# Scores as one float32 product each, and two more projection units in seven products: a neighbourhood-attention layer on one Trainium2 core

## The chip, the cores and the metric

The kernel runs on one core of one Trainium2 chip, in one launch. The metric is the device time of that launch in microseconds. The engines are named as the profile names them: PE (matrix products), PEld (loading of a product's stationary operand), DVE (vector), ACT (scalar activation), POOL (GpSimd), SP (the queue that issues most DMAs).

## The reference

One layer of a transformer trunk over 2048 tokens of width 1024 that form a grid of 32 rows by 64 columns: RMS norm, one input projection into queries, keys, values and a gate, 2-D neighbourhood attention with 16 heads of 64, SiLU gate, output projection, residual, final RMS norm. All is float32.

```python
h = rmsnorm(x, norm_0)
q, k, v, gate = split(h @ w_in_0, 4)                  # 2048 x 1024 each
# query (r, c) sees 8 rows x 16 columns of keys around it, clipped at the border
s = q . k / sqrt(64) + rpb[head, row offset, column offset]
o = softmax(s) @ v
x = x + (o * silu(gate)) @ w_out_0
out = rmsnorm(x, norm_f)
```

## The kernel before

**Products.** Large products run as three float32r products, high by high, high by low and low by high: an operand is copied into float32r by ACT (the high half) and the difference to the copy is formed by DVE (the low half). The `o` products of attention (L1123) take float32 operands whole.

**Stage one** projects the first 1024 tokens, **stage two** the other 1024. A block of columns of queries, keys or gate (a unit: 256 output columns, 1024 tokens) is either made by `group` (L378 to L382: per 128 columns and 512 tokens 8 x 3 products, 96 for a unit's 1024 tokens) or by `seven_products` (L434): a Strassen-like scheme with 7 instead of 8 block products, 7 x 12 = 84 products, and additions on DVE (`s`, `u`, `tmp`). Values are made by `values_of` (L555). Before, stage two does six units with seven products (`units_two`); the other six (`halves`) are made by `group` later, as filling between attention's steps.

**Stores between stages.** `give` takes a finished block. Queries go to `qd`, the gate through tanh to `sgd`. Of keys ACT makes a high copy (L364) and DVE the low rest (L365), and both are stored, in `k_hi` and `k_lo`. `store` puts a DMA into a list with a due time that is counted in products (`clock`); `due` issues what has come due.

**The attention stage** has 32 cycles, one for each pair of heads p and row tile T (8 x 64 queries). `order` gives first all pairs with T = 0, then each pair with T = 1 and 2, then all with T = 3. The keys of a tile span 11, 15, 15 and 12 rows. In cycle m PE runs, in this order: some filling products (`feed`), the transposes of the last cycle's probabilities (`turns`, L1101), two calls of `scores` (L1021) and two of `values` (L1123, tile `o`). `scores` handles a pair of column blocks; for each column block and each of the two heads, which sit in the lower and upper 64 partitions, it computes

```python
for m, (qq, kk) in enumerate(((qh, kh), (qh, kl), (ql, kh))):
    for s in range(2):
        a = slice(s * 64, s * 64 + 64)
        nc.tensor.matmul(pst[s], qq[a, qs], kk[a, :r1 - r0, c0:c1].rearrange("p r (s c) -> p s r c", c=8), ...)
```

Then DVE adds the bias table and takes the row maximum (L1029), ACT takes the exponential (L1035), DVE the reciprocal of the sums (L1040), and `normalise` multiplies on POOL (L1044). The bias tables `em` are sums made on POOL (L987). `split_q` (L519, L520) makes the halves of the queries, scaled by 1/8, from the loaded tile `qr`.

**Filling.** `amount[m]` is the number of products that `feed` takes in cycle m: 28 in the first 25 cycles, the rest spread over the last seven. The filling is first `projections` (the remaining units by `group`), then `outputs` (L1322 to L1326), the output projection, whose operand rows are split by `split_og` (L1187, L1188). `consume` splits the next weights on ACT and DVE (L189, L190).

Of the kernel before, what the change touches and what calls it, by code (L numbers as in the profile page):

```python
# [70 lines left out]
def build(ctx, tc, x, xr, xt, wg, rpb, last, w_out, n0, nf, masks, out):  # L71
# [4 lines left out]
    k_hi = [dram.tile([128, S], F32, name=f"k_hi{p}") for p in range(NP)]  # L76
    k_lo = [dram.tile([128, S], F32, name=f"k_lo{p}") for p in range(NP)]
# [53 lines left out]
    rt = one.tile([128, 16], F32, name="rt")  # L131
    g0 = one.tile([128, NK], F32, name="g0")
# [25 lines left out]
    def load_item(it):  # L158
        kind, a, b = it
        t = raws[it] = raw([128, 512], F32, "raw")  # L160
        asked_at[it] = clock[0]
# [44 lines left out]
    def stats(c):  # L206
        ss = rows.pop(c)
        m = tiny.tile([128, 8], F32, name="m")[:, :4]
        nc.vector.tensor_tensor(m, ss[:, 0:8:2], ss[:, 1:8:2], OP.add)
        nc.vector.tensor_scalar(m, m, 1.0 / D, EPS, op0=OP.mult, op1=OP.add)  # L210
        rsqrt(rt[:, 4 * c:4 * c + 4], m, 4)

# [32 lines left out]
    units_two = [(k, j) for j in range(2) for k in "kqg"]  # L245
    halves = [(k, j, 1, c) for j in range(2, 4) for g in (("k", "q", "g") if j == 2 else ("k", "qg")) for c in (2, 3) for k in g]
# [16 lines left out]
    clock = [0.0]  # L263
    freed = set()
# [23 lines left out]
    def consume(n, asked=False, turn=False):  # L288
        for _ in range(n):
            load_ahead()  # L290
            if attending[0] and not asked and not turn:
                return
            if state["used"] == len(items) or not may_use(items[state["used"]]):
                return
            if attending[0] and clock[0] - asked_at[items[state["used"]]] < 32 and not asked:
                return
            it = items[state["used"]]
            state["used"] += 1
            use_item(it)
# [44 lines left out]
    def give(kind, hp, c, t, bank_=False):  # L344
        while sum(e[1][0] in "kqg" for e in later) > 1:
            later.pop(0)[2]()
        s = slice(c * 512, c * 512 + 512)
        written.add((kind, hp, c))
        to, at = (lambda o: lay(kind, o), of(kind, t)) if bank_ else (lambda o: o, t)
        if kind == "g":  # L350
            sg = ev([128, 512], F32, "sg")
            nc.scalar.activation(to(sg), at, AF.Tanh, scale=0.5)
            nc.vector.scalar_tensor_tensor(to(sg), to(sg), 1.0, at, op0=OP.add, op1=OP.mult)
            store(("g", hp, c), 12, lambda: nc.sync.dma_start(sgd[hp][:, s], sg))
            return
        if kind == "q":
            if bank_:
                t = ev([128, 512], F32, "q")
                nc.scalar.activation(to(t), at, AF.Copy)
            store(("q", hp, c), 12, lambda: nc.sync.dma_start(qd[hp][:, s], t))  # L360
            return
        hi = ev([128, 512], F32R, "hi")
        lo = ev([128, 512], F32R, "lo")
        nc.scalar.activation(to(hi), at, AF.Copy)  # L364
        nc.vector.tensor_tensor(to(lo), at, to(hi.bitcast(F32)), OP.subtract)  # L365
        store(("k", hp, c), 12, lambda: (nc.sync.dma_start(k_hi[hp][:, s], hi.bitcast(F32)),
                                         nc.sync.dma_start(k_lo[hp][:, s], lo.bitcast(F32))))
# [20 lines left out]
    def evac_v(u, t, p):  # L388
        v = ev([128, 512], F32, "v")
        nc.scalar.activation(v, p, AF.Copy, scale=rt[:, t:t + 1] if t < 8 else 1.0)  # L390
# [140 lines left out]
    def split_v(u, a, b, ks=(0, 1)):  # L531
        t = VR[u, a, b].rearrange("p (k c) -> p k c", c=256)
        if a == 0 and ks[0] == 0:
# [3 lines left out]
        nc.scalar.activation(h, t[:, k], AF.Copy)  # L537
# [28 lines left out]
    def stage_one():  # L566
# [119 lines left out]
        for k in range(NK):  # L686
            if k == 0:
                for h in range(2):
                    split_to(*(t[:, parts_[h]] for t in X1["B11"][0]), land["x11"][0][:, parts_[h]], gain("x11", 0))
                    if h == 0:  # L690
                        split_v(0, 0, 0, (0,))
                        split_v(0, 1, 0, (0,))
# [93 lines left out]
    def stage_two():  # L786
# [9 lines left out]
        def also(n, i):  # L796
            if n == 0:
# [12 lines left out]
                if i == 3:  # L810
                    for f in load_k(0, 0) + [load_q(0, 0)]:
                        f()
                if i == 5:
                    split_q(0, 0)
# [117 lines left out]
    def load_k(p, T):  # L932
# [3 lines left out]
        KT[p, T] = []  # L936

        def keys(src):
            t = kp([128, 960], F32R, "kt")
            KT[p, T].append(t.rearrange("p (r c) -> p r c", c=GW))  # L940
            nc.sync.dma_start(t[:, :n].bitcast(F32), src[p][:, r0 * GW:r1 * GW])

        return [lambda: keys(k_hi), lambda: keys(k_lo)]

    def load_q(p, T):
        must(("q", p, T))

        def queries():
            QT[p, T] = t = lp([128, 512], F32, "qr")
            nc.sync.dma_start(t, qd[p][:, T * 512:T * 512 + 512])  # L950

        return queries

    def split_q(p, T):
        t = QT[p, T]
        QT[p, T] = h, l = qp([128, 512], F32R, "qh"), qp([128, 512], F32R, "ql")
        split_to(h, l, t, HD ** -0.5)
# [50 lines left out]
    def scores(i, between=None):  # L1008
        p, T, cs = pairs[i]
        kh, kl = KT[p, T]  # L1010
        qh, ql = QT[p, T]
        r0, r1 = KEY_ROWS[T]
        got = []
        for C in cs:
# [3 lines left out]
            for m, (qq, kk) in enumerate(((qh, kh), (qh, kl), (ql, kh))):  # L1018
                for s in range(2):
                    a = slice(s * 64, s * 64 + 64)  # L1020
                    nc.tensor.matmul(pst[s], qq[a, qs], kk[a, :r1 - r0, c0:c1].rearrange("p r (s c) -> p s r c", c=8), start=(m == 0), stop=(m == 2))  # L1021
# [16 lines left out]
    def normalise(i):  # L1038
        st = ST.pop(i)
        nc.vector.reciprocal(st[:, 8:12], st[:, 4:8])  # L1040
        for j, C in enumerate(pairs[i][2]):
            for s in range(2):
                o = 8 + 2 * j + s
                nc.gpsimd.tensor_scalar(X[i, C][s], X[i, C][s], st[:, o:o + 1], 0.5, op0=OP.mult, op1=OP.mult)  # L1044
# [236 lines left out]

    def outputs():
        loaded_at = {1: -1e9}
# [5 lines left out]
        def ahead(k, i=0):  # L1289
            n = ready["loaded"]  # L1290
            if n < tiles and place[n] <= k + 4 and og_ready(n):
                load_og(n)
                loaded_at[n] = clock[0]
# [4 lines left out]
            near = 2 if quiet[0] else -1  # L1298
            if n < ready["loaded"] and place[n] <= k + near and clock[0] - loaded_at[n] >= 28 and whole(n):
# [38 lines left out]
    dense, end_of_it = 28.0, 24  # L1338
# [3 lines left out]
    amount[1] += first  # L1342
    calm_debt = dense / 4
# [34 lines left out]
    def begin(m):  # L1378
# [6 lines left out]
        if m + 1 < cycles:  # L1385
            nx = order[m + 1]
            if nx[1] == 3:
                later_loads(load_last(nx[0]), 12, 1.5)
            later_loads(load_k(*nx), 14 if nx[1] < 3 else 22, 5)
# [3 lines left out]

    def middle(m):
        if 1 <= m < cycles:
            split_q(*order[m])
        if m + 1 < cycles:
            later_loads([load_q(*order[m + 1])], 1, 0)
# [12 lines left out]
    for m in range(cycles + 1):  # L1411
        a = amount[m]
        begin(m)
        feed(a * 0.35)
        if m:
            normalise(2 * m - 1)
        middle(m)
        if m:
            quiet[0] = True
            for k in range(3):  # L1420
                consume(1 + (m == 1), turn=True)
                feed(a * 0.11)
# [4 lines left out]
            if quiet[0]:  # L1427
                consume(1, turn=True)
                feed(a * 0.12)
                quiet[0] = False  # L1430
            else:
                feed(a * 0.12)
        else:
            feed(a * 0.45)
        feed(a * 0.2, 8)
# [12 lines left out]
        if m:  # L1448
            values(2 * m - 2)
            values(2 * m - 1)  # L1450
        n = next_sums(m)
# [55 lines left out]
```

## Time and profile before

| | |
|---|---|
| median of 3 runs | 1062.33 us (1062.28 to 1062.53) |
| the profiled execution's own time | 1062.42 us |
| span of its trace | 1060.6 us |
| PE busy | 1048.6 us, 99% of the span |
| DVE, ACT, POOL busy | 725.7, 518.5, 312.9 us |
| granted TensorE clock, mean | 0.999 |
| DMA | 207.58 MB, 196 GB/s |
| attention stage | from about 531 us to about 1005 us |

The trace covers the span; some 1.8 us of the profiled execution lie outside it. Busy shares are averages over stages; what bounds a stage is read from PE's timeline and from what PE waits for.

### The profile page before, as it was taken

What the parts mean: (1) busy time and instruction counts of PE and PEld (TensorE: products, weight loads), DVE (VectorE), ACT (ScalarE), POOL (GpSimd) and SP (SyncE); (2) the same over time, 40 slices, a digit from 0 to 9 for tenths busy, and PEclk for the clock granted to TensorE, in tenths of its full rate; (3) what the DMA queues carried; (4) which work ended last, traced back from release to release, by engine and by line L of the source; (5) the groups of instructions that cost most, each with busy time, mean ns of one, the idle gap of its engine ahead of it and who ended that gap; (6) DMA issues with size and microseconds to landing.
All of it is one profiled execution on the core that took longest, in us unless ns stands there. A gap on an engine that the chain in (4) does not pass through costs nothing.

```text
span 1060.6 us, 20997 instructions
## 1 busy us (share of the span) xinstructions
PE 1048.6 (99%) x7608; PEld 877.1 (83%) x7608; DVE 725.7 (68%) x1593; ACT 518.5 (49%) x1218; POOL 312.9 (30%) x392
## 2 busy tenths in 40 slices
PE   8999999999999999999999999999999999999997
PEld 6888888887888888888888888888887888888886
DVE  5476888768897625666576667766778777686654
ACT  7645344333343334333265656666767656445422
POOL 0000221322311000000157775665756642213200
PEclk9999999999999999999999999999999999999999
DMA  8733655353635433533798778886987788777352
GB/s 309 227 100 108 190 202 179 126 149 119 184 120 154 120 100 89 170 99 129 234 300 262 239 238 246 269 268 207 297 280 251 222 282 273 255 243 247 105 155 80
DMA packets 129184, 207.58 MB, mean 196 GB/s; under 512 B 11768, under 2 KB 55544, under 8 KB 129080
## 3 DMA queue, kind: packets, MB, share of 16 engines
q1 hardware_dynamic: 128648, 205.84, 62.5%
q8 instruction: 60, 0.98, 0.4%
q10 hardware_dynamic: 432, 0.40, 0.1%
q14 instruction: 44, 0.36, 0.1%
HBM read 147.47 MB, written 58.72 MB: 194 GB/s over the span
## 4 chain that ended last, share of the span: by engine, by line
PE 91%; DVE 4%; issue 1%; POOL 1%; DMA 1%; ACT 0%; SPq 0%; POOLq 0%; DVEq 0%
PE pp L434 30%; PE pv L555 16%; PE s L1021 7%; PE o L1123 7%; PE po L1324 5%; PE po L1326 5%; PE po L1322 5%; PE pp L382 4%; PE pp L378 4%; PE pp L380 4%; PE ph L1101 4%; DVE f L417 1%; POOL x L1044 1%; DMA land<-in_xt_dram 1%; POOL em L987 1%
## 5 line engine op out<-in xcount | busy, mean ns | idle before, releaser
L1044 POOL TENSOR_SCALAR x<-x,st 128x360 f32<-128x360 f32 (+5 forms) x256 | 176.1, 706 | 222.9 <-DVE st L1040 205.0
L434 PE MATMUL pp<-h,f 128*128 128x512 f32 x576 | 186.6, 390 | 0.0
L1035 ACT ACTIVATE x<-x,st 128x360 f32<-128x360 f32 (+5 forms) x256 | 151.3, 593 | 23.7 <-DVE st L1029 23.7
L454 POOL TENSOR_TENSOR tmp<-tmp,rb 128x512 f32<-128x512 f32 x36 | 58.6, 1628 | 270.1 <-DVE tmp L452 209.4
L987 POOL TENSOR_TENSOR em<-e,mk 128x264 f32<-128x264 f32 (+3 forms) x94 | 78.0, 864 | 192.1 <-DMA mk<-in_masks_dram 189.4
L434 PEld LDWEIGHTS pp<-h,f 128*128 128x128 f32 x576 | 108.2, 188 | 22.2
L1029 DVE CUSTOM_DVE_ANT_0 x<-s,em 128x360 f32<-128x360 f32 (+5 forms) x256 | 123.8, 538 | 0.6 <-POOL em L987 0.6
L434 PE MATMUL pp<-t,f 128*128 128x512 f32 x480 | 121.7, 390 | 0.3
L434 PE MATMUL pp<-l,f 128*128 128x512 f32 x288 | 112.2, 389 | 0.0
L434 PEld LDWEIGHTS pp<-t,f 128*128 128x128 f32 x480 | 90.0, 188 | 19.6 <-DVE u L447 1.1
L1324 PE MATMUL po<-woh,gl 128*128 128x512 f32 x252 | 99.2, 394 | 1.5 <-DVE gl L1188 1.5
L1326 PE MATMUL po<-wol,gh 128*128 128x512 f32 x252 | 98.9, 393 | 0.0
L1322 PE MATMUL po<-woh,gh 128*128 128x512 f32 x252 | 98.9, 393 | 0.0
L1077 DVE COPY pta<-ph 120x512 f32<-120x512 f32 (+5 forms) x96 | 57.8, 641 | 55.4 <-PE ph L1101 55.4
L555 PE MATMUL pv<-wh,h 128*128 128x512 f32 x256 | 88.4, 391 | 1.9 <-ACT h L519 1.4
L555 PE MATMUL pv<-wh,l 128*128 128x512 f32 x256 | 88.2, 390 | 0.0
L555 PE MATMUL pv<-wl,h 128*128 128x512 f32 x256 | 88.2, 390 | 0.0
L1077 ACT ACTIVATE pta<-ph 120x512 f32<-120x512 f32 (+5 forms) x96 | 49.7, 558 | 77.0 <-PE ph L1101 76.8
L1123 PEld LDWEIGHTS o<-pta,vt 120*64 120x64 f32 (+2 forms) x1792 | 80.9, 138 | 7.4 <-DVE st L1029 5.4
L1123 PE MATMUL o<-pta,vt 120*64 120x128 f32 (+5 forms) x1792 | 85.3, 253 | 0.0
L417 DVE TENSOR_TENSOR f<-raw,f 128x512 fp32r<-128x512 f32 x90 | 69.7, 775 | 22.4 <-ACT f L416 22.4
L1021 PE MATMUL s<-kt,qh 64*128 64x480 f32 (+5 forms) x512 | 83.0, 372 | 0.5 <-DVE pta L1077 0.5
(157 smaller groups left out, 1959.5 us busy)
## 6 DMA issues: line engine op xcount, KB each, us to landing
raw<-in_wg_dram SPq DMA_DIRECT2D x126, 256.0 KB, 5.0
row<-in_xr_dram SPq DMA_DIRECT2D x32, 256.0 KB, 4.0
vd<-v SPq DMA_DIRECT2D x32, 256.0 KB, 2.4
k_hi<-hi SPq DMA_DIRECT2D x32, 256.0 KB, 2.5
k_lo<-lo SPq DMA_DIRECT2D x32, 256.0 KB, 2.9
sgd<-sg SPq DMA_DIRECT2D x32, 256.0 KB, 4.1
qr<-qd SPq DMA_DIRECT2D x32, 256.0 KB, 5.0
sgt<-sgd SPq DMA_DIRECT2D x32, 256.0 KB, 5.1
```

Source lines behind the costliest of these rows:

```text
L434: nc.tensor.matmul(B[n, P], t[:, int(m == 2), c], x[k][int(m == 1)], start=P in (1, 6, 5) and k == 0 and m == 0, stop=k == 3 and m == 2, s ...
L555: nc.tensor.matmul(ps[t], a[:, o], b, start=k == 0 and m == 0, stop=k == NK - 1 and m == 2)
L987: (nc.gpsimd if attending[0] or not s else nc.vector).tensor_tensor(sh(t), E[p, s][:, u0 + 4:u1 + 4, v0 + 8:v1 + 8].rearrange("p u (s v) - ...
L1021: nc.tensor.matmul(pst[s], qq[a, qs], kk[a, :r1 - r0, c0:c1].rearrange("p r (s c) -> p s r c", c=8), start=(m == 0), stop=(m == 2))
L1029: nc.vector.tensor_tensor_reduce(X[i, C][s], pst[s], EM[p, ROW_TYPE[T], COL_TYPE[C], s], -1.0, 1e38, OP.add, OP.min, st[:, o:o + 1])
L1035: nc.scalar.activation(X[i, C][s], X[i, C][s], AF.Exp, bias=st[:, o:o + 1], scale=-1.0, accum_out=st[:, 4 + o:5 + o])
L1044: nc.gpsimd.tensor_scalar(X[i, C][s], X[i, C][s], st[:, o:o + 1], 0.5, op0=OP.mult, op1=OP.mult)
L1077: (nc.vector.tensor_copy if h else lambda o, i_: nc.scalar.activation(o, i_, AF.Copy))(t[:k, h, b * 512:b * 512 + w], banks_[b, h][:k, :w])
L1123: nc.tensor.matmul(to.rearrange("d (h q) -> d h q", q=64) if nq > 64 else to, vt[:k, strip, s * 64:s * 64 + 64], t[:k, h, at:at + 64] if n ...
L1322: nc.tensor.matmul(p, gh, woh[q, j], start=(i == 0), stop=False)
L1324: nc.tensor.matmul(p, gl, woh[q, j], start=False, stop=False)
L1326: nc.tensor.matmul(p, gh, wol[q, j], start=False, stop=(i == NK - 1))
```

## The change

- `scores`: one float32 product for each column block and head, in place of three float32r products. Keys and queries stay whole: one store `kd`, one load per tile; `split_q` and `middle` go; queries are scaled by 1/8 when they are stored.
- Stage two: eight units by `seven_products` (`k` and `q` of the third column are added), so four by `group` in the attention stage. The filling of the first 25 cycles falls from 28 to 20.3 products a cycle (plus or minus 1.5 in turn in cycles 8 to 23).
- `normalise` of the second pair multiplies its second column block on ACT. The factor 0.5, which stood in that multiply, moves into the store of the values (`rth`).
- The cycle feeds 10 products before that `normalise`, and the rest in other shares. The rows of the output projection are split by `split_rows` in the quiet places of a cycle, at most three turns ahead.
- Start: DVE in place of ACT converts one of the first value weights; two loads are cut in halves and interleaved with those of x.
- Times of loads are counted with `now()`, which adds 26 products for each cycle run.

```diff
-    units_two = [(k, j) for j in range(2) for k in "kqg"]
-    halves = [(k, j, 1, c) for j in range(2, 4) for g in (("k", "q", "g") if j == 2 else ("k", "qg")) for c in (2, 3) for k in g]
+    units_two = [(k, j) for j in range(2) for k in "kqg"] + [(k, 2) for k in "kq"]
+    halves = [(k, j, 1, c) for j in range(2, 4) for g in (("g",) if j == 2 else ("k", "qg")) for c in (2, 3) for k in g]
...
+        if bank_:
+            t = ev([128, 512], F32, kind)
+            nc.scalar.activation(to(t), at, AF.Copy, scale=HD ** -0.5 if kind == "q" else 1.0)
+        elif kind == "q":
+            nc.scalar.activation(t, t, AF.Copy, scale=HD ** -0.5)
+        store((kind, hp, c), 12, lambda: nc.sync.dma_start((qd if kind == "q" else kd)[hp][:, s], t))
...
         for b in (1, 2, 3):
-            for a in range(2):
-                load_v0(0, a, b, ev([128, 512], F32, "raw") if b == 3 else None)
-            for k in (2 * b, 2 * b + 1):
-                load("x%d1" % (k // 4 + 1), k % 4)
+            for j in range(2):
+                for a in range(2):
+                    if b == 1:
+                        load_v0(0, a, b, cols=parts_[j])
+                    elif j == 0:
+                        load_v0(0, a, b, ev([128, 512], F32, "raw") if b == 3 else None)
+                load("x%d1" % (b // 2 + 1), (2 * b + j) % 4)
...
-            for m, (qq, kk) in enumerate(((qh, kh), (qh, kl), (ql, kh))):
-                for s in range(2):
-                    a = slice(s * 64, s * 64 + 64)
-                    nc.tensor.matmul(pst[s], qq[a, qs], kk[a, :r1 - r0, c0:c1].rearrange("p r (s c) -> p s r c", c=8), start=(m == 0), stop=(m == 2))
+            for s in range(2):
+                a = slice(s * 64, s * 64 + 64)
+                nc.tensor.matmul(pst[s], qt[a, qs], kt[a, :r1 - r0, c0:c1].rearrange("p r (s c) -> p s r c", c=8), start=True, stop=True)
...
-                nc.gpsimd.tensor_scalar(X[i, C][s], X[i, C][s], st[:, o:o + 1], 0.5, op0=OP.mult, op1=OP.mult)
+                if both and j:
+                    nc.scalar.activation(X[i, C][s], X[i, C][s], AF.Copy, scale=st[:, o:o + 1])
+                else:
+                    nc.gpsimd.tensor_scalar(X[i, C][s], X[i, C][s], st[:, o:o + 1], 1.0, op0=OP.mult, op1=OP.mult)
...
+    def split_rows():
+        n = ready["split"]
+        if n < ready["loaded"] and "turn" in ready and place[n] <= ready["turn"] + 3 and now() - late["loaded_at"][n] >= 40 and whole(n) \
+                and sum(1 if hasattr(g, "rearrange") else 2 for g in G.values()) <= 6:
+            split_og(n)
+            ready["split"] += 1
+            return True
...
-    dense, end_of_it = 28.0, 24
+    dense, end_of_it = 20.3, 24
...
+    for m in range(8, 24):
+        amount[m] += 1.5 if m % 2 == 0 else -1.5
...
+            later_loads([load_q(*nx), load_k(*nx)], 7, 5)
...
-        a = amount[m]
+        a = amount[m] - 10
         begin(m)
-        feed(a * 0.35)
+        feed(10)
         if m:
-            normalise(2 * m - 1)
-        middle(m)
+            normalise(2 * m - 1, True)
         if m:
             quiet[0] = True
             for k in range(3):
-                consume(1 + (m == 1), turn=True)
-                feed(a * 0.11)
+                if not split_rows():
+                    consume(1 + (m == 1), turn=True)
+                feed(a * 0.17)
```

More of the change, by code (lines that the diff above doesn't have):

```diff
@@ L75, in build @@
     qd = [dram.tile([128, S], F32, name=f"qd{p}") for p in range(NP)]
-    k_hi = [dram.tile([128, S], F32, name=f"k_hi{p}") for p in range(NP)]
-    k_lo = [dram.tile([128, S], F32, name=f"k_lo{p}") for p in range(NP)]
+    kd = [dram.tile([128, S], F32, name=f"kd{p}") for p in range(NP)]
     sgd = [dram.tile([128, S], F32, name=f"sgd{p}") for p in range(NP)]
@@ L131, in build @@
     rt = one.tile([128, 16], F32, name="rt")
+    rth = one.tile([128, 8], F32, name="rth")
     g0 = one.tile([128, NK], F32, name="g0")
@@ L263, in build, with now @@
     clock = [0.0]
+    runs = [0]
+    def now():
+        return clock[0] + 26 * runs[0]
     freed = set()
@@ L294, in consume @@
                 return
-            if attending[0] and clock[0] - asked_at[items[state["used"]]] < 32 and not asked:
+            if attending[0] and now() - asked_at[items[state["used"]]] < 36 and not asked:
                 return
@@ L935, in load_k, with keys @@
         must(*[("k", p, c) for c in range(r0 // 8, (r1 + 7) // 8)])
[L936 to L943, printed above, removed]
+        def keys():
+            t = kp([128, 960], F32, "kt")
+            KT[p, T] = t.rearrange("p (r c) -> p r c", c=GW)
+            nc.sync.dma_start(t[:, :n], kd[p][:, r0 * GW:r1 * GW])
+        return keys
     def load_q(p, T):
@@ L1036, in scores, with normalise @@
                                      accum_out=st[:, 4 + o:5 + o])
-    def normalise(i):
+    def normalise(i, both=False):
         st = ST.pop(i)
@@ L1297, in ahead @@
             n = ready["split"]
-            near = 2 if quiet[0] else -1
-            if n < ready["loaded"] and place[n] <= k + near and clock[0] - loaded_at[n] >= 28 and whole(n):
+            ready["turn"] = k
+            if ended[0] and n < ready["loaded"] and place[n] <= k + 2 and now() - loaded_at[n] >= 28 and whole(n):
                 split_og(n)
@@ L1450, in build @@
             values(2 * m - 1)
+        runs[0] += 1
         n = next_sums(m)
```

72 lines of the change are left out of this document (27 added, 45 removed).

## The prediction

> **What bounds the kernel now.** I read the page first: the busy times and the chain that ended last.
>
> ```profile
> span 1060.6 us, 20997 instructions
> PE 1048.6 (99%) x7608; PEld 877.1 (83%) x7608; DVE 725.7 (68%) x1593; ACT 518.5 (49%) x1218; POOL 312.9 (30%) x392
> PE 91%; DVE 4%; issue 1%; POOL 1%; DMA 1%; ACT 0%; SPq 0%; POOLq 0%; DVEq 0%
> ```
>
> PE is 99% busy and is 91% of the chain. So the time is the sum of what PE streams, plus the few places where PE waits. I therefore read PE's own timeline, start to start, because ends are modelled. Columns: start us, length us.
>
> ```profile
> 606.61 0.39 PE L382 MATMUL pp<-h,w 128*128 128x512 f32 x1
> 612.51 0.39 PE L380 MATMUL pp<-l,w 128*128 128x512 f32 x1
> 612.82 1.43 PE L1101 MATMUL ph<-ident,x 64*88 64x64 f32 x44
> 614.06 0.55 PE L1021 MATMUL s<-kt,qh 64*128 64x264 f32 x3
> 616.42 2.67 PE L1123 MATMUL o<-pta,vt 88*64 88x128 f32 x56
> 619.01 0.51 PE L382 MATMUL pp<-h,w 128*128 128x512 f32 x1
> 665.65 0.74 PE L1021 MATMUL s<-kt,qh 64*128 64x360 f32 x4
> 668.56 0.66 PE L1123 MATMUL o<-pta,vt 120*64 120x128 f32 x8
> 894.62 0.71 PE L1021 MATMUL s<-kt,qh 64*128 64x288 f32 x4
> 897.12 2.67 PE L1123 MATMUL o<-pta,vt 96*64 96x128 f32 x56
> ```
>
> Between the first two rows lie 26 float32r products: 5.90/26 = 0.227 us each, 0.443 ns per column. A score block (all four column blocks of one head pair and row tile) takes 616.42 - 614.06 = 2.36 us where the tile has 11 key rows, 668.56 - 665.65 = 2.91 us with 15, and 897.12 - 894.62 = 2.50 us with 12. There are 8, 16 and 8 such blocks: 18.9 + 46.6 + 20.0 = 85.4 us. The block of `o` products takes 619.01 - 616.42 = 2.59 us, and the transposes 614.06 - 612.82 = 1.24 us.
>
> Where PE waits is in the waits by engine (total us, times, longest):
>
> ```profile
> PE po L1324 <- DVE gl L1188: 1.5, 2, 1.1
> PE pv L555 <- ACT h L519: 1.4, 1, 1.4
> PEld pp L434 <- DVE u L447: 1.1, 2, 0.6
> ```
>
> So little is to be won from waits. The change is decided by PE's own work.
>
> **Two more units by seven products.** `units_two` grows from six to eight. A unit costs 7 x 12 = 84 products in this form and 96 in `group`. That is 2 x 12 = 24 products less, at 0.227 us: -5.4 us. The additions that it costs instead lie on DVE, which has room where that stage runs; I cost them at nothing.
>
> **The scores.** Each is one float32 product where there were three float32r products. No float32 score is in this trace, so I need a price from other float32 work. The products by form show how many records one product leaves (count | busy us, mean ns):
>
> ```profile
> L1021 PE MATMUL s<-kt,qh 64*128 64x480 f32 x128 | 25.1, 417 | 0.4 <-DVE pta L1077 0.4
> L1021 PE MATMUL s<-kt,ql 64*128 64x480 f32 x64 | 18.5, 412 | 0.0
> L1123 PE MATMUL o<-pta,vt 120*64 120x128 f32 x512 | 38.9, 276 | 0.0
> ```
>
> The 16 blocks with 15 key rows have 4 scores of 480 columns each, 64 in all: 192 records, three per score, one per float32r product. The `o` products are float32 already. The same 16 blocks hold 16 of 128 columns each, 256 in all, and leave 512 records: two passes per float32 product.
>
> One `o` block has 16 products of 128 columns and 12 of 64, spread over two halves of the output's partitions that run side by side. Each half therefore streams 16 x 128 + 12 x 64 = 2816 columns in its two passes, in 2.59 us: 0.920 ns per column and pass, 2.08 times the 0.443 of float32r. A second row is the transposes, float32 in one pass on the two halves of the input's partitions, as the scores are: 22 x 64 = 1408 columns in 1.24 us, 0.881 ns. The two agree, with switching between blocks included.
>
> A head's score block has 112 key columns times 11, 15 or 12 rows: 1232, 1680 and 1344 columns. Two passes at 0.920 make 2.27, 3.09 and 2.47 us against 2.36, 2.91 and 2.50 now. With 8, 16 and 8 blocks that is 18.1 + 49.5 + 19.8 = 87.4 us, +1.9. At the transposes' 0.881 the blocks would take 2.17, 2.96 and 2.37 us, 83.7 us in all: -1.7, the lower bound.
>
> The upper bound comes from how slowly float32r runs in this place now:
>
> ```profile
> 666.28 0.82 PE L1021 MATMUL s<-kt,qh 64*128 64x480 f32 x4
> 667.03 0.81 PE L1021 MATMUL s<-kt,qh 64*128 64x480 f32 x4
> ```
>
> From the first score block of 480 columns to the second, 0.75 us pass for three products per head: 0.521 ns per column, where 0.443 is paid elsewhere. Something here (runs of eight keys, or two streams at once) stretches a pass. If a float32 product costs four such passes, the blocks grow by one third of what lies in them: 0.521 x 1232, 1680 and 1344 ns = 0.64, 0.88 and 0.70 us, or 8 x 0.64 + 16 x 0.88 + 8 x 0.70 = +24.8 us. I take +1.9: both float32 rows are near it, and a stretch of a stream that runs at half speed has time to hide.
>
> The Trainium skill (FP8 and Floating Point Precision, TensorE Precision Notes) says that true FP32 takes four passes through the array. The two records at 2.08 times the float32r column agree with that, 4.16 in all. By that rule with each pass priced as a score pass now, the sum would be the upper bound and not +1.9.
>
> **What becomes lighter beside PE.** Key halves and query halves are no longer formed, and the low halves are neither stored nor loaded:
>
> ```profile
> L365 DVE TENSOR_TENSOR lo<-tmp,hi 128x512 fp32r<-128x512 f32 x22 | 15.0, 682 | 5.5 <-ACT hi L364 5.5
> L520 DVE SCALAR_TENSOR_TENSOR ql<-qr,qh 128x512 fp32r<-128x512 f32 x32 | 26.1, 815 | 16.9 <-ACT qh L519 14.1 <-DMA ogd<-og 2.0 <-DMA e<-in_rpb_dram 0.3
> L519 ACT ACTIVATE qh<-qr 128x512 fp32r<-128x512 f32 x32 | 19.8, 618 | 0.0
> k_lo<-lo SPq DMA_DIRECT2D x32, 256.0 KB, 2.9
> 280.00:320.00 40.00, 40.00 (x178) 33.13 (x178) 37.26 (x51) 14.76 (x26) 9.84 (x6) 1.00 0.44 134
> ```
>
> All this lies beside PE, so its direct worth is nothing. The last row (a window: PE, PEld, DVE busy) shows DVE at 37.26 of 40 us in the first seven-product stage; without `lo` it has slack, and I let the waits of PE behind `u` go: -0.6 us. ACT now scales the queries, where the first stage stored them as they came; it is busy 14.76 of 40 there and hides that. SP issues one key load per block instead of two; the load of queries moves from 1 to 7 products into a cycle and that of keys from 14 to 12, both for the cycle after, so nothing near waits for them.
>
> **The start.** The change cuts the two loads of the second value weights in halves, and puts the second halves behind the next tile of x. ACT works in order, and `split_v` of these weights stands before the split of that tile.
>
> ```profile
> 9.93 0.63 ACT L537 ACTIVATE wh<-raw 128x512 fp32r<-128x512 f32 x1 [1.43 <-DMA raw<-in_wg_dram]
> 11.41 1.41 ACT L519 ACTIVATE h<-land,g 128x512 fp32r<-128x512 f32 x2 [0.85 <-DMA land<-in_xt_dram]
> 12.18 1.20 PE L555 MATMUL pv<-wh,h 128*128 128x512 f32 x4 [1.38 <-ACT h L519]
> ```
>
> Now x lands last, at 11.41, and PE starts 0.77 us later. After the change weights land last, at about the same time, since the bytes are the same, and one or two weight splits of 0.63 us stand between that and x: +0.6 to +1.3, or -0.7 if half the bytes of a load decide. I take +0.7. The earlier first product (DVE takes one of the first conversions) ends in this same wait and is worth nothing.
>
> **The dense cycles.** In 25 cycles of the attention stage 20.3 products fill the time between the blocks instead of 28; the total stays, since two units moved ahead. So each cycle is 7.7 x 0.227 = 1.75 us shorter, and ACT, DVE and POOL have that much less time. Two of eight `normalise` multiplies per cycle move to ACT.
>
> ```profile
> 638.70:858.10 219.40, 217.39 (x2444) 186.28 (x2441) 161.14 (x434) 144.59 (x378) 135.22 (x173) 1.00 0.82 252
> L1044 POOL TENSOR_SCALAR x<-x,st 128x480 f32<-128x480 f32 x64 | 52.0, 826 | 11.8 <-DVE st L1040 10.7
> ```
>
> The 16 cycles of the window take 13.7 us each, with DVE 10.1, ACT 9.0 and POOL 8.5 busy. After it a cycle is 13.7 - 1.75 + 0.18 = 12.1; DVE loses 0.8 (`ql`), ACT loses 0.6 and gains some 1.2, POOL loses two multiplies of 0.83: 9.3, 9.6, 6.8 at most. All fit. PE's 2.0 us of waits there include the 1.5 behind `gl`; the output rows are now split earlier (two ACT copies and two DVE subtractions each, in place of a weight split), so I let these 1.5 go and set 1.5 against them for cycles with less slack: nothing in sum.
>
> **Sum.** -5.4 + 1.9 - 0.6 + 0.7 = -3.4 us. The profiled execution took 1062.4 us (span 1060.6), 0.1 above the median 1062.3. So 1059.0 against it, and 1058.9 as a median. About 0.2%, 2.1 us, is what a measurement of this kernel can tell from no change.
>
> **Rivals.** *Stretched passes (slower).* Float32 scores carry the stretch of float32r in this place. For it: the same operands in the same runs of eight, and 0.521 against 0.443. Against it: the transposes use the same input halves at 0.881. In full it gives -3.4 + 24.8 - 1.9 = +19.5, 1082; with half the difference 1070. It decides from +1.9 + 3.4 = 5.3 us more than now, 6% on the block. The Trainium skill (SBUF — State Buffer, SBUF: two separate sides) says that a read wants two hits per 16-byte line; runs of eight float32 meet that, which speaks against this rival, but no run here shows it.
>
> *A late normalise (slower).* The transposes wait for `normalise`, which now waits in ACT's queue behind the exponentials and a fill's evacuation.
>
> ```profile
> 655.12 0.33 PE L1123 MATMUL o<-pta,vt 120*64 120x128 f32 x2
> 658.40 0.58 ACT L1035 ACTIVATE x<-x,st 128x360 f32<-128x360 f32 x1
> 661.49 2.64 POOL L1044 TENSOR_SCALAR x<-x,st 128x480 f32<-128x480 f32 x4 [2.17 <-DVE st L1040]
> 664.33 1.39 PE L1101 MATMUL ph<-ident,x 64*120 64x64 f32 x39
> ```
>
> Exponentials end 3.9 us after the scores; two multiplies on POOL (1.7) reach 5.6; PE gets to the transposes after 2.59 + 20.3 x 0.227 = 7.2, against 9.2 here. Slack 1.6 us; in this cycle POOL began 2.5 us after the exponentials, which would overrun it by 0.9. If half of 25 cycles do: +11, 1070.
>
> *Better than forecast.* Transposes' price for the scores, and the 1.5 us behind `gl` won without new waits: -3.4 - 3.6 - 1.5, 1054.
>
> **Chances.** Forecast 0.50, stretched passes 0.24, late normalise 0.14, better 0.12. The forecast's own spread (1056 to 1062) puts a quarter of it within 0.2%. So faster 0.48, same 0.15, slower 0.37. The range takes the better case and both rivals at half price: 1053 to 1074; stretched passes in full are left out. The forecast's own range is 1056 to 1062.
>
> **What would show it.** Score blocks of about 2.27, 3.09 and 2.47 us, with two records per score. 24 products fewer in stage two and the fill. PE's first long wait some 0.7 us longer, none behind `gl`. Transposes that follow the fill without a gap. The prediction is wrong if score blocks exceed 3.3 us with 15 key rows, or if PE's busy share in the dense cycles falls below 97%.

## The result, and the profile after

The changed kernel took 1074.6 us (median of 5 runs, 1069.29 to 1075.61) against 1062.28 (1061.06 to 1062.53) for the kernel before: a ratio of 1.0111, interval 1.0086 to 1.0137. It is slower; the forecast was 1058.9. The profiled execution took 1075.17 us, its span 12.3 us more than before.

The page of the changed kernel, busy times and shares of the chain:

```profile
span 1072.9 us, 20176 instructions
PE 1053.9 (98%) x7328; PEld 859.5 (80%) x7328; DVE 699.3 (65%) x1556; ACT 535.5 (50%) x1254; POOL 256.1 (24%) x328
PE 92%; DVE 3%; ACT 2%; issue 1%; DMA 1%; SPq 0%; DVEq 0%; ACTq 0%
```

PE runs 280 fewer instructions and is busy 5.3 us longer. DVE and POOL are busy less, as predicted; no engine became the bound. Summed from PE's timeline, from the start of one record to the start of the next, so that a wait ahead of a block counts to what ran before it:

| us | before | after | |
|---|---|---|---|
| products of queries, keys, gate | 479.1 | 472.5 | -6.6 |
| products of values | 176.0 | 176.9 | +0.9 |
| scores | 87.1 | 101.7 | +14.7 |
| transposes | 41.5 | 46.2 | +4.7 |
| `o` products | 83.0 | 83.1 | 0 |
| output rows (`po`) | 180.2 | 179.3 | -0.9 |
| other products (`zp`, `prb`) | 6.1 | 5.8 | -0.3 |

The waits of PE (total us, times, longest):

```profile
PE s L1019 <- DVE pta L1078: 5.3, 2, 4.5
PE s L1019 <- DVE y L1221: 2.9, 1, 2.9
PE pv L559 <- ACT h L520: 1.4, 2, 1.2
PE zp L124 <- DVE z L121: 1.2, 1, 1.2
PE s L1019 <- DVE sg L360: 1.2, 1, 1.2
PE po L1333 <- DVE gl L1189: 0.6, 1, 0.6
```

The wait behind `gl` has shrunk from 1.5 to 0.6. New are waits ahead of or inside score blocks, 9.4 us in all and all for DVE. Undisturbed score blocks, from PE's timeline (start, length):

```profile
642.91 2.58 PE L1019 MATMUL s<-kt,q 64*128 64x264 f32 x16
645.42 2.67 PE L1124 MATMUL o<-pta,vt 88*64 88x128 f32 x56
...
714.16 3.17 PE L1019 MATMUL s<-kt,q 64*128 64x360 f32 x16
717.26 0.99 PE L1124 MATMUL o<-pta,vt 120*64 120x128 f32 x16
...
1001.22 2.72 PE L1019 MATMUL s<-kt,q 64*128 64x288 f32 x16
1003.87 0.88 PE L1124 MATMUL o<-pta,vt 96*64 96x128 f32 x14
```

A block takes 2.51 us with 11 key rows, 3.10 with 15 and 2.65 with 12; eight scores leave 16 records, two each. All 32 blocks at these lengths are 20.1 + 49.6 + 21.2 = 90.9 us, 5.5 more than before. The other 9 of the 14.7 us are waits and what follows a wait. The largest lies here (DVE, POOL, ACT, then PE; an idle time before an entry and its releaser stand in brackets):

```profile
734.72 7.00 DVE L195 TENSOR_TENSOR wol<-raw,woh 128x512 fp32r<-128x512 f32 x3 [1.80 <-ACT woh L194]
741.65 1.74 DVE L1078 COPY pta<-ph 120x512 f32<-120x512 f32 x3
...
730.85 3.70 POOL L1045 TENSOR_SCALAR x<-x,st 128x360 f32<-128x360 f32 x6 [8.12 <-DVE st L1027]
734.51 5.46 POOL L987 TENSOR_TENSOR em<-e,mk 128x360 f32<-128x360 f32 x6
...
733.09 1.07 ACT L1043 ACTIVATE x<-x,st 128x360 f32<-128x360 f32 x2
734.06 1.67 ACT L194 ACTIVATE woh<-raw 128x512 fp32r<-128x512 f32 x3
...
735.64 1.51 PE L1102 MATMUL ph<-ident,x 64*120 64x64 f32 x44
736.98 0.90 PE L1019 MATMUL s<-kt,q 64*128 64x360 f32 x4
742.38 4.09 PE L1019 MATMUL s<-kt,q 64*128 64x480 f32 x12 [4.50 <-DVE pta L1078]
746.40 2.71 PE L1124 MATMUL o<-pta,vt 120*64 120x128 f32 x56
```

ACT does its two new multiplies (733.09) and only then splits the weights (734.06). POOL has only six multiplies left and starts the sums of the bias tables at 734.51. So DVE's three subtractions and POOL's six sums run at the same time. Each reads two tiles from SBUF. The subtractions take 7.00 us where three alone take 2.05 (0.684 each). One of them lasts 5.8 us, through all six sums. The copies that empty the PSUM banks of the transposes (`pta`, L1078) stand behind them on DVE, and PE cannot write the next scores: PE's last pass ends at 737.87, and PE stands for 4.5 us until 742.38. The block that follows is slow too. Windows of that stretch (PE, PEld, DVE, ACT, POOL busy, granted clock, DMA share, GB/s):

```profile
737.70:742.30 4.60, 0.17 (x2) 0.00 (x0) 4.60 (x5) 0.30 (x1) 2.27 (x3) 1.00 0.16 45
742.40:746.40 4.00, 4.00 (x13) 1.51 (x13) 4.00 (x13) 2.53 (x9) 0.00 (x0) 0.59 0.95 309
```

After 4.5 us of standing the granted clock is 0.59 over the next 4 us. Starts of two successive passes, first at full clock and then in that stretch, from PE's timeline:

```profile
714.83 1.10 PE L1019 MATMUL s<-kt,q 64*128 64x480 f32 x4
715.23 1.10 PE L1019 MATMUL s<-kt,q 64*128 64x480 f32 x4
...
743.45 1.81 PE L1019 MATMUL s<-kt,q 64*128 64x480 f32 x4
744.25 1.61 PE L1019 MATMUL s<-kt,q 64*128 64x480 f32 x4
```

They lie 0.40 us apart, then 0.80. This score block takes 9.42 us in place of 3.10. The Trainium skill (TensorE: Matmul & The Clock Gate, What's actually happening) says that the array falls to half clock after an idle window of some 3.4 us. The half clock agrees (0.50 from 743.5 to 746.4). A wait of that length is not needed here: one of 2.9 us, at 792.7, was followed by 0.50 too (798 to 800), and so was one of 2.6 us in the run of the multiplies alone, below (753 to 757).

A second place, at 788 (DVE, POOL):

```profile
788.15 5.50 DVE L1189 TENSOR_TENSOR gl<-ograw,gh 128x512 fp32r<-128x512 f32 x4 [1.67 <-ACT gh L1188]
793.57 1.35 DVE L195 TENSOR_TENSOR wol<-raw,woh 128x512 fp32r<-128x512 f32 x1
...
787.92 7.72 POOL L987 TENSOR_TENSOR em<-e,mk 128x360 f32<-128x360 f32 x6
```

Here the two engines take turns: five subtractions take 6.8 us, and six sums 7.7. The transposes run from 791.21 to 792.71, and then PE stands for 2.9 us until DVE has done `y`, which lies behind the subtractions; the score block that follows takes 5.83 us. In the table this wait, and another of 1.2 us, count to the transposes: they are 4.0 of the +4.7 there. In the kernel before, the same work lay apart (DVE, POOL):

```profile
660.52 0.69 DVE L365 TENSOR_TENSOR lo<-pp,hi 128x512 fp32r<-128x512 f32 x1 [2.00 <-ACT hi L364]
661.22 0.66 DVE L520 SCALAR_TENSOR_TENSOR ql<-qr,qh 128x512 fp32r<-128x512 f32 x1
665.08 1.83 DVE L1077 COPY pta<-ph 120x512 f32<-120x512 f32 x3 [3.20 <-PE ph L1101]
...
661.49 2.64 POOL L1044 TENSOR_SCALAR x<-x,st 128x480 f32<-128x480 f32 x4 [2.17 <-DVE st L1040]
664.11 4.64 POOL L987 TENSOR_TENSOR em<-e,mk 128x360 f32<-128x360 f32 x5
```

The subtractions are done when POOL reaches the sums, and DVE then only copies from PSUM, at 0.61 us each. Counted over the attention stage, subtractions that overlap a table sum: 4 before, of which two are lengthened (0.73 and 1.20 us), and 24 after, with a median of 1.19 us (0.68 to 5.80). Those of weights and output rows beside POOL's multiplies (46 before) keep a median of 0.684, the same as those beside nothing; but 20 of the 46 take 0.77 to 1.15 us, and of those beside nothing none takes more than 0.70.

### The profile page after: what moved, and what is told of

The parts are those of the page before. It is cut to its first block, busy times and chain, and to the rows that moved or that the text cites. A ratio compares the mean times of both kernels' runs of the same rounds, so it can differ in the third digit from the quotient of the medians.

```text
span 1072.9 us, 20176 instructions
## 1 busy us (share of the span) xinstructions
PE 1053.9 (98%) x7328; PEld 859.5 (80%) x7328; DVE 699.3 (65%) x1556; ACT 535.5 (50%) x1254; POOL 256.1 (24%) x328
## 4 chain that ended last, share of the span: by engine, by line
PE 92%; DVE 3%; ACT 2%; issue 1%; DMA 1%; SPq 0%; DVEq 0%; ACTq 0%
PE pp L435 34%; PE pv L559 16%; PE s L1019 9%; PE o L1124 7%; PE po L1333 5%; PE po L1335 5%; PE po L1331 5%; PE ph L1102 4%; PE pp L383 2%; PE pp L381 2%; PE pp L379 2%; ACT x L1033 1%; DMA raw<-in_wg_dram 1%; DVE x L1027 0%; DVE f L418 0%
## 5 line engine op out<-in xcount | busy, mean ns | idle before, releaser
L435 PE MATMUL pp<-h,f 128*128 128x512 f32 x640 | 207.1, 389 | 0.0
L1045 POOL TENSOR_SCALAR x<-x,st 128x480 f32<-128x480 f32 (+5 forms) x192 | 110.5, 593 | 252.8 <-DVE st L1038 227.0
L987 POOL TENSOR_TENSOR em<-e,mk 128x264 f32<-128x264 f32 (+3 forms) x94 | 87.0, 960 | 230.2 <-DMA mk<-in_masks_dram 226.0
L435 PEld LDWEIGHTS pp<-h,f 128*128 128x128 f32 x640 | 120.1, 188 | 24.8
L435 PE MATMUL pp<-t,f 128*128 128x512 f32 x532 | 135.0, 389 | 0.1
L435 PE MATMUL pp<-l,f 128*128 128x512 f32 x320 | 124.5, 389 | 0.0
L435 PEld LDWEIGHTS pp<-t,f 128*128 128x128 f32 x532 | 99.8, 188 | 21.2 <-DVE u L448 0.6
L1019 PE MATMUL s<-kt,q 64*128 64x480 f32 (+5 forms) x512 | 98.7, 503 | 9.4 <-DVE pta L1078 5.3
L418 DVE TENSOR_TENSOR f<-raw,f 128x512 fp32r<-128x512 f32 x100 | 73.1, 731 | 40.5 <-ACT f L417 40.5
L1124 PEld LDWEIGHTS o<-pta,vt 120*64 120x64 f32 (+2 forms) x1792 | 80.9, 137 | 14.7 <-DVE st L1027 13.2
L1078 DVE COPY pta<-ph 120x512 f32<-120x512 f32 (+5 forms) x96 | 57.3, 639 | 47.5 <-PE ph L1102 47.5
L1019 PEld LDWEIGHTS s<-kt,q 64*128 64x128 f32 x512 | 63.0, 190 | 30.1 <-DVE pta L1078 10.7
```

Of the source, the lines that this page charges most:

```text
L418: nc.vector.tensor_tensor(t[:, 1], src, t[:, 0].bitcast(F32), OP.subtract)
L435: nc.tensor.matmul(B[n, P], t[:, int(m == 2), c], x[k][int(m == 1)], start=P in (1, 6, 5) and k == 0 and m == 0, stop=k == 3 and m == 2, s ...
L987: (nc.gpsimd if attending[0] or not s else nc.vector).tensor_tensor(sh(t), E[p, s][:, u0 + 4:u1 + 4, v0 + 8:v1 + 8].rearrange("p u (s v) - ...
L1019: nc.tensor.matmul(pst[s], qt[a, qs], kt[a, :r1 - r0, c0:c1].rearrange("p r (s c) -> p s r c", c=8), start=True, stop=True)
L1124: nc.tensor.matmul(to.rearrange("d (h q) -> d h q", q=64) if nq > 64 else to, vt[:k, strip, s * 64:s * 64 + 64], t[:k, h, at:at + 64] if n ...
```

## The experiments

The theories in the expectations: **A**, DVE's subtractions run against POOL's table sums, because two multiplies moved from POOL to ACT; **B**, the float32 scores bring the waits; **C**, the shortened cycle is too short in itself; **D**, ACT's two multiplies cost by the time that they take on ACT. Ratios are against the kernel before, run beside each.

**Scores alone.** The kernel before with only the float32 scores and the keys and queries kept whole.

```diff
-            for m, (qq, kk) in enumerate(((qh, kh), (qh, kl), (ql, kh))):
...
+                nc.tensor.matmul(pst[s], qt[a, qs], kt[a, :r1 - r0, c0:c1].rearrange("p r (s c) -> p s r c", c=8), start=True, stop=True)
```

> The kernel before with the float32 scores alone (whole keys and queries, one store and load), six units, 28 products, normalise on POOL. Score blocks as in the changed kernel: 2.51, 3.10 and 2.65 us, 90.9 us against 85.4 before. Theory A (the scores cost 5 us, the rest of the loss is DVE subtractions that run against POOL's table sums): 1067, no wait over 1 us in the attention stage beyond those of before. Theory B (the float32 scores bring the long waits, by their length or by the loads): 1070 or more with waits of PE in the cycles.

1064.35 us, ratio 1.0022 (1.0012 to 1.0032). The scores take 91.4 us, +4.3, with clean blocks of 2.51, 3.10 and 2.66 and no wait above 1 us in the attention stage. B is out: the scores cost their own 4 to 5 us and no more, and the kernel gets some of it back, so that it is 2.7 us faster than the 1067 of theory A.

**Units alone.** The kernel before with eight units by seven products, 20.3 products a cycle (with the plus or minus 1.5), and the times of loads counted with `now()`.

```diff
+    units_two = [(k, j) for j in range(2) for k in "kqg"] + [(k, 2) for k in "kq"]
...
+    dense, end_of_it = 20.3, 24
```

> The kernel before with eight units by seven products and 20.3 products a cycle, float32r scores, normalise on POOL, the feed shares of before. 24 products fewer are -5.4 us. Theory A: the tables still run after the weight splits, 1056 to 1058. Theory C (a cycle shorter by 1.75 us is too short for ACT, DVE and POOL whatever their order): waits remain, 1062 or more.

1063.78 us, 1.0016 (1.0006 to 1.0025): not the gain of 5. Transposes, with the waits that follow them, took 46.7 us (+5.2) and scores, still float32r, 91.4 (+4.3). PE's waits:

```profile
PE ph L1106 <- POOL x L1049: 1.7, 4, 0.7
PE s L1026 <- DVE y L1225: 1.6, 1, 1.6
...
PE s L1026 <- ACT pta L1082: 1.2, 2, 0.8
```

So a weak form of C fits: with all the splitting still in it, the kernel with the short cycle gives the saving back. That it is the cycle's length, and not the changed times of the loads, was not tested apart.

**All multiplies on POOL.** The changed kernel with one line put back.

```diff
-            normalise(2 * m - 1, True)
+            normalise(2 * m - 1)
```

> The changed kernel with all eight multiplies of normalise on POOL. Theory A: POOL reaches the tables some 1.3 us later and ACT reaches the weight splits 1.1 us earlier, so the two overlap less: 1060 to 1066, DVE subtractions back to 0.7 us. Theory C: POOL's chain gets longer in a cycle that is too short, transposes wait more: 1075 or more.

1061.71 us, 0.9996 (0.9987 to 1.0005): 13 us less than the changed kernel, from one line. DVE, POOL and ACT in a like place:

```profile
731.23 2.31 DVE L195 TENSOR_TENSOR wol<-raw,woh 128x512 fp32r<-128x512 f32 x3 [0.82 <-ACT woh L194]
...
728.05 6.38 POOL L1045 TENSOR_SCALAR x<-x,st 128x360 f32<-128x360 f32 x8 [5.15 <-DVE st L1038]
734.40 0.87 POOL L987 TENSOR_TENSOR em<-e,mk 128x360 f32<-128x360 f32 x1
...
730.58 1.66 ACT L194 ACTIVATE woh<-raw 128x512 fp32r<-128x512 f32 x3
```

Counted from the start of this cycle's `o` products (726.44 here, 728.49 in the changed kernel), ACT starts the weight splits 1.4 us earlier and POOL the tables 1.9 us later. The subtractions lie beside POOL's multiplies at 0.77 us each, and the tables come after them. A and D both survive this.

**No tables.** The changed kernel without the table sums of pairs 1 to 7 in the first three row tiles (those tables are left out of the computation).

```diff
+            if p and ty < 2:
+                for cty in range(3):
+                    for s in range(2):
+                        EM[p, ty, cty, s] = EM[0, ty, cty, s]
+            else:
+                for cty in range(3):
+                    bias(p, ty, cty)
```

> The changed kernel without the table sums of head pairs 1 to 7 for the first three row tiles (their scores use the tables of pair 0, so the bias of the other pairs is left out). Theory A: nothing on POOL meets the subtractions, the waits of 5, 3 and 1 us go: 1057 to 1062. Theory C: the multiplies on ACT and the short cycle remain, 1068 or more.

1059.79 us, 0.9978 (0.9969 to 0.9987). The multiplies are on ACT as in the changed kernel, and 14.8 us are gone; transposes are back at 41.8. The weight subtractions (min/median/max ns) here, in the changed kernel, and with all multiplies on POOL:

```profile
L195 DVE TENSOR_TENSOR wol<-raw,woh x16: 683/686/693, 720.6 to 805.7; 128x512 fp32r<-128x512 f32 x16
...
L195 DVE TENSOR_TENSOR wol<-raw,woh x16: 677/686/5800, 722.9 to 820.0; 128x512 fp32r<-128x512 f32 x16
...
L195 DVE TENSOR_TENSOR wol<-raw,woh x16: 677/714/1102, 718.8 to 805.2; 128x512 fp32r<-128x512 f32 x16
```

None of these exceeds 0.693 us without the sums. Since the multiplies are still on ACT here, D is out for any large part; A stands.

**ACT only where no tables are made.** As above with the tables kept.

```diff
-            normalise(2 * m - 1, True)
+            normalise(2 * m - 1, m == cycles or order[m][1] >= 2)
```

> The changed kernel with the two multiplies on ACT only in cycles that build no tables (second of each two from cycle 8 on, and the last row tile); elsewhere all eight on POOL. Theory A (DVE subtractions against POOL's table sums): nothing new overlaps, and the transposes' waits for POOL (2.7 us with all on POOL) shrink in half of the cycles: 1059 to 1062, at or below all on POOL (1061.7). Theory D (the two multiplies on ACT cost by themselves, since they stand ahead of the weight splits in ACT's queue): a loss remains in half of the cycles, 1065 or more.

1061.14 us, 0.9992 (0.9983 to 1.0001): again 13 us less than the changed kernel, and not to be told from all multiplies on POOL.

**The multiplies alone.** The kernel before with only the two multiplies moved to ACT (and the factor 0.5 to the values).

```diff
+                if both and j:
+                    nc.scalar.activation(X[i, C][s], X[i, C][s], AF.Copy, scale=st[:, o:o + 1])
```

> The kernel before with only the two multiplies of the second pair on ACT (and the factor 0.5 moved into the values' store). Cycles stay long, 28 products. Theory A in its strong form (the move alone makes tables and subtractions meet): POOL is at the tables 1.4 us earlier, subtractions of 1.2 us and more while tables run, 1065 or more. If the short cycles are needed as well: subtractions may lengthen, but PE has slack, 1060 to 1063.

1076.26 us, 1.0127 (1.0113 to 1.0141). The move alone, in the long cycle of 28 products and with float32r scores, costs all of it and a little more: 44 subtractions overlap table sums, at a median of 1.21 us. On PE the loss lies in other places than in the changed kernel: scores +5.9, output rows +5.6, transposes +2.7. DVE, POOL, PE in one place:

```profile
747.71 4.37 DVE L196 TENSOR_TENSOR wol<-raw,woh 128x512 fp32r<-128x512 f32 x3
752.00 1.74 DVE L1083 COPY pta<-ph 120x512 f32<-120x512 f32 x3
...
746.35 7.27 POOL L990 TENSOR_TENSOR em<-e,mk 128x360 f32<-128x360 f32 x6
...
752.73 1.17 PE L1024 MATMUL s<-kt,qh 64*128 64x480 f32 x4 [2.64 <-DVE pta L1083]
```

The strong form of C (that the loss needs the short cycle) is out.

**A longer cycle.** The kernel with ACT only where no tables are made, at 22.5 products.

```diff
-    dense, end_of_it = 20.3, 24
+    dense, end_of_it = 22.5, 24
```

> As act_norm_where_no_tables, with 22.5 instead of 20.3 products in the 25 dense cycles and fewer in the last seven, the total unchanged. A cycle is 0.5 us longer. If what is left of the waits comes from short cycles (Theory C in its weak form), these go: 1057 to 1060. If not, the same time as act_norm_where_no_tables.

1077.24 us, 1.0147 (1.0133 to 1.0161), with two long waits that none of the theories named:

```profile
PE po L1331 <- ACT gh L1188: 9.0, 1, 9.0
PE s L1019 <- DVE pta L1078: 5.1, 2, 4.8
```

The filling ran out of rows of the output projection (9.0 us). The other wait, of 4.8 us, ends behind DVE's scaling of a finished output row (L1241 to L1253), which ran beside table sums from 816.3 on: steps on single columns that take 0.16 to 0.22 us elsewhere took up to 1.02. This says nothing on the weak C; it shows that one such meeting, late in a cycle, is enough.

**Float32r scores again.** The kernel with ACT only where no tables are made, with three float32r products per score and the halves split, and the loads of keys and queries timed, as before.

> As act_norm_where_no_tables, with three float32r products per score, halves of keys and queries stored, loaded and split as before. Score blocks back at 2.36, 2.91 and 2.50 us, 4 to 5 us less on PE than with float32. If DVE and ACT have room for the splits: 1055 to 1058. If the splits bring the waits that eight units alone had (PE +7 us of waits): 1060 to 1064; then the float32 scores earn their 5 us of PE by what they take off DVE and ACT.

1064.14 us, 1.0016 (1.0007 to 1.0025), 3.0 us more than with float32 scores.

```profile
PE ph L1119 <- POOL x L1062: 2.5, 6, 0.7
PE s L1036 <- ACT pta L1095: 1.5, 2, 0.8
```

Clean score blocks are shorter (2.35, 2.93, 2.51), but waits fill the score line up to 90.9, and transposes take 46.8. So in the short cycle the float32 scores earn their 4 to 5 us back. That they do so by what they take off DVE and ACT fits these waits, but was not tested apart from the times of the loads.

**POOL early, ACT late.** Two kernels part the move: one leaves the two multiplies out (that block stays unnormalised), so POOL is early and ACT not late; the other does all eight on POOL and two idle ones on ACT, so only ACT is late.

```diff
-                    nc.scalar.activation(X[i, C][s], X[i, C][s], AF.Copy, scale=st[:, o:o + 1])
+                    pass
```
```diff
+                    nc.scalar.activation(junk[:, :w], junk[:, :w], AF.Copy, scale=st[:, o:o + 1])
+                nc.gpsimd.tensor_scalar(X[i, C][s], X[i, C][s], st[:, o:o + 1], 1.0, op0=OP.mult, op1=OP.mult)
```

> The changed kernel without the two multiplies that went to ACT (the second column block of each second pair stays unnormalised). POOL is at the tables as early as in the changed kernel, ACT at the weight splits 1.1 us earlier than there. If POOL's early start alone makes tables and subtractions meet: subtractions of 1.2 us and more remain, 1068 or more. If ACT's delay is needed: 1059 to 1062.

> The changed kernel with all eight multiplies on POOL and, in ACT's queue where two of them stood, two multiplies of a scratch tile that wait for the same reciprocals. ACT is as late as in the changed kernel, POOL as late as with all on POOL. If ACT's delay alone makes them meet: 1066 or more. If POOL's early start is needed: 1061 to 1064.

Early POOL: 1060.66 us, 0.9983 (0.9974 to 0.9992). Late ACT: 1066.66 (1064.31 to 1070.34), 1.0047 (1.0029 to 1.0066). In both, subtractions meet sums (15 at a median of 1.07 us, 16 at 1.10). Early POOL costs nothing, so meetings alone are no loss. Late ACT alone costs some 5 us: PE's score blocks wait 3.0 us for DVE in its trace, which is that of its fastest run, against 0.8 us with early POOL. Neither half gives the 13 us. What goes with the loss, by a count over the traces and not by an experiment, is how late in the cycle the meetings lie. Meetings that end more than 1 us after the cycle's transposes have begun are 8 in the changed kernel, 9 with the multiplies alone, 6 with late ACT, 1 with early POOL, and none in the kernel before or with all multiplies on POOL.

**A one-source subtraction.** The changed kernel with the low halves as `h` times a constant, one source in place of two (the low part is left out of the products).

```diff
-            nc.vector.tensor_tensor(l, t, h.bitcast(F32), OP.subtract)
+            nc.vector.tensor_scalar(l, h.bitcast(F32), 2.0 ** -13, None, op0=OP.mult)
```

> The changed kernel with the low half of output weights, late projection weights and output rows made by DVE from one source (a multiple of the high half, so the low part of these operands is left out). Theory A (a subtraction that reads two tiles in SBUF takes turns with POOL's sums, which do too): if two sources are what collides, the operations keep one duration beside the tables and the waits go: 1058 to 1063. If any DVE operation between SBUF tiles collides: 1068 or more.

1066.01 us (1063.65 to 1069.83), 1.0043 (1.0024 to 1.0062).

```profile
L190 DVE TENSOR_SCALAR w<-w x16: 419/709/1156, 552.1 to 660.7; 128x512 fp32r<-128x512 f32 x16
L195 DVE TENSOR_SCALAR wol<-woh x16: 420/428/1323, 721.1 to 810.0; 128x512 fp32r<-128x512 f32 x16
```

The time lies between the two that were expected. The shorter instruction meets the sums too: 0.43 us alone, a median of 0.99 over 26 meetings. That a second source is needed for the collision is not borne out. The loss shrinks by some 8 us; that this is because the instruction is shorter was not tested. A subtraction that reads one operand from PSUM (`lo` from `pp`) is another matter: in the traces of four kernels (the one before, units alone, float32r scores again, multiplies alone) it meets the sums eight times in all and takes 0.68 to 0.69 us each time.

**All together.** ACT only where no tables are made, the order of loads at the start as before, and 3.0 products in turn in place of 1.5.

```diff
-        amount[m] += 1.5 if m % 2 == 0 else -1.5
+        amount[m] += 3.0 if m % 2 == 0 else -3.0
```

> As act_norm_where_no_tables, with 3.0 instead of 1.5 products moved from the cycles without tables to those with (cycles 8 to 23), and the loads of the start in the order of before. The transposes' waits in the cycles with tables (some 2 us) shrink, and PE's first long wait is 0.9 us shorter if the cut loads cost it: 1057 to 1060. If neither matters: 1061.

1060.68 us (1060.07 to 1062.83), 0.9993 (0.9983 to 1.0002). Its median is 1.1 us under the kernel before, inside what can be told. Of the versions that compute everything, none is measurably faster than the kernel before.

## Why the prediction was wrong

**The units.** Right. 24 products fewer were to give -5.4; the line gave -6.6. The rest fits the -0.6 put down for waits behind `u`: in the trace they fell from 1.1 to 0.6 us in total, though no run tested that part alone.

**The scores.** Right mechanism, wrong size: +1.9 forecast, +5.5 by clean blocks (+4.3 as the sum of the scores-alone kernel). Two records per score, as said. No stretch: two passes of 480 columns start 0.40 us apart, 0.84 ns per column, less than the 0.920 used. But blocks cost a part besides, 0.28 to 0.44 us: 1232 columns in two passes at 0.84 are 2.07 us of 2.51, 1680 are 2.82 of 3.10, 1344 are 2.26 of 2.65. The `o` block had spread its switching over 2816 columns; for 15 rows the two errors cancel (3.09 forecast, 3.10 measured), so that agreement is luck, and for shorter blocks they do not (2.27 and 2.51, 2.47 and 2.65). The four passes of the Trainium skill (FP8 and Floating Point Precision, TensorE Precision Notes) agree in price (0.84 is 1.9 times 0.443, twice); the rival that hung on it, stretched passes, did not happen.

**The start.** Right in mechanism: PE's long wait was to end 0.7 us later. It ends at 12.72 where it was 12.18, +0.5; ACT's split of a weight at 11.42 now stands ahead of its split of x at 11.96. The wait itself is no longer (1.2 us, 1.4 before), since PE reaches it later. And the first product of a unit starts at 95.5 where it was 94.9, +0.6. This start scatters: 94.3 to 95.0 over the kernels with the old order of loads, 93.9 to 96.6 over those with the new one, so the sign is likely and the size is not settled.

**The dense cycles.** This step failed. The prediction set DVE's, ACT's and POOL's busy time against the cycle, found that "All fit", and put 0 us. All did fit: POOL's busy time fell from 312.9 to 256.1 us. What moved was the order in time. Two multiplies fewer bring POOL to its table sums sooner, two more bring ACT to the weight splits later, and DVE's subtractions follow ACT. The prediction looked at each queue by itself and never asked what would then run beside what. The price of two instructions side by side was not in the sum. The runs put this term, forecast at 0 us, at 13 us: 1074.6 against 1061.7 with the two multiplies back on POOL. The trace of before shows only two lengthened meetings (0.73 and 1.20 us). PE's busy share from 568 to 778.7 is 204.27 of 210.70 us, 96.9%, just under the 97% that was named as the sign of being wrong.

**The rival "late normalise"** had the sign, the instruction and nearly the time (1070), but not the waiter; that its time came near is luck. It had the transposes waiting for ACT. In fact the score blocks wait for DVE, and taking away the table sums, with the multiplies still on ACT, removes the loss.

**What the collision hides.** With all multiplies on POOL the change is worth -0.4 us, not to be told from nothing, where -3.4 was forecast. The terms there: scores +5.0, transposes +2.7, against -6.5 of products and small gains elsewhere. So about 3 us more than forecast went into the score term and about 2.7 into transposes, which wait in some of the shorter cycles and, undisturbed, take 0.03 us more each beside float32 scores.

The meeting itself, its partners and its effect on PE are shown by the no-tables run, the move alone, and the one line put back. What decides whether DVE is held through one sum (1.2 us) or through six (5.8 us) stays open, and so does what puts the meetings late enough in a cycle to cost PE time.

## What to carry to other kernels

When work moves from one engine to another, draw the new order in time of all engines and look for pairs that slow each other, not only for engines that run full. Keep POOL's two-tile sums away from DVE's subtractions, above all late in a cycle, where DVE's next job frees a PSUM bank for PE. The part that each block costs besides its columns belongs in the price of a short block; a price per column taken from a long one leaves it out.

## What the runs showed of the hardware

- A DVE subtraction of 128x512 float32, two tiles from SBUF, takes 0.684 us alone. Beside POOL's multiplies by a per-row factor 26 of 46 keep that in the kernel before, and 20 take 0.77 to 1.15; the multiplies give way as well (with all on POOL, eight take 4.9 us alone in the middle cycles and 5.3 to 7.2 beside subtractions). Beside POOL's sums of two tiles most take 0.8 to 1.6, and one took 5.8. With one operand in PSUM it took 0.68 to 0.69 in eight such meetings (traces of four kernels). The Trainium skill (SBUF — State Buffer, Who interferes with whom) says that a DVE instruction with two SBUF inputs contends with a GpSimd instruction that reads SBUF, and that the first to issue holds the ports while the other blocks. The sums and the multiplies agree; the one of 5.8 us was held through six sums of the other engine, not one.
- PE, after standing for 4.5 us, ran at a granted clock of 0.59 for the next 4 us: one late copy cost 6.3 us of score block. Waits of 2.9 and 2.6 us were followed by a granted clock of 0.50 too.
- Float32 score passes run at 0.84 ns per column with runs of eight keys, where float32r passes there take 0.521 against 0.443 elsewhere: the stretch does not carry over.
